# Gates as columns of the first value group, rows by transposes, and five low parts a layer by ScalarE and an adding DMA, in a two-layer hybrid block

## The chip, the cores and the metric

The kernel runs on one core of a Trainium2 chip. The metric is the time of one execution on the device in microseconds, here the median of the runs. One further execution is recorded by the hardware profiler; it has a time of its own, and a span, which goes from the first to the last instruction.

## The reference

Two layers, each a hybrid mixer and a feed-forward part with a convolution, on 512 positions of width 1024. The parts that matter here, cut:

```python
for l in range(2):
    x = x + rms_norm(hybrid_mixer(rms_norm(x, mix_pre_g[l]), w_in[l], ...), mix_post_g[l])
    x = x + rms_norm(conv_ffn(rms_norm(x, ffn_pre_g[l]), ...), ffn_post_g[l])

def hybrid_mixer(hn, w_in, ...):
    # attention q, k, v: 512 columns each; mLSTM q, k, v, o: 512 each; gates: 16
    aq, ak, av, mq, mk, mv, mo, gates = split(hn @ w_in)
    attn = dilated_attention(rotary(aq), rotary(ak), av)          # 8 heads of 64
    mq, mk = silu(depthwise_conv(concat(mq, mk)))
    g = gates + mlstm_gate_b                                      # input and forget gates, 2 directions, 4 heads
    h = mlstm(mq, mk, mv, g, forward) + mlstm(mq, mk, mv, g, backward)
    return concat(attn, rms(h) * head_g * sigmoid(mo)) @ w_out

def conv_ffn(hn, w_up, conv_w, conv_b, w_down):                   # 1024 -> 2 x 2816 -> 1024
    gate, val = split(depthwise_conv(hn @ w_up))
    return (gelu(gate) * val) @ w_down
```

## The kernel before

**Products.** Activations lie with features on partitions and the 512 positions in the free dimension. Each large product is made of three passes in rounded fp32: a number is split in a high part (rounded) and a low part (the rest), and TensorE adds high x high, low x high and high x low. `mac` (L230 to L232) does that for one k-tile of 128: three matmuls with weights standing and 512 positions moving, or 256 where a group is done by halves of the positions.

**Weights** come as 104 pieces a layer (`plan`): 28 of w_in, 8 of w_out, 44 of w_up, 24 of w_down, 512 KB each (128 x 1024). `load_raw` lets SyncE load a piece to `wraw`; `split_w` lets ScalarE cast it to `whi` (L183) and VectorE subtract (`wlo = wraw - whi`, L115). `take` hands the next piece on, and `prefetch(n)` splits up to n pieces ahead, where the code calls it. whi and wlo have rings of three.

**The order of a layer.** `ORDER` gives, for each of four rounds, the order of the mLSTM q and k, the attention q (a) and k (b), and the values (V, two pieces). V has the positions standing and 256 weight columns moving (L923 to L925). `rot_out` turns a and b, `conv_out` does the mLSTM convolution, `v_out` scales V. Two streams (`A` attention, `M` mLSTM with `gates` first) are interleaved with the macs by rates. Beyond that a scheduler fixes each engine's order at build time; an engine then works strictly in its order.

**The first group** of a layer's mixer (`mixer_first`) runs before the norm's scale is known, and the scale is applied to its results. In layer 0 it is gates, q and k for all positions; in layer 1 it follows the feed-forward part of layer 0 and goes by halves, so that the first half starts while the second half of x is still being made; then a is done whole. The gates are products of their own (`gate_macs`, L484 and L486: 16 columns with their low parts as 32 standing columns) in a bank `gps`; `gates` copies them and transposes them (L546).

**The norms.** `Stats` collects squares; `flush` sums them over partitions by small matmuls (L344), `rstd` and `rsqrt_cols` make 1/root on VectorE (rs_y, L282 to L296), `row_of` turns a column into a row spread over all partitions: two fp32 matmuls with `ident_rs`, the identity times 1/RS, since rs_y carries a factor RS (L359). `Post.finish` multiplies that row into the branch (mg or fg, L432), adds it to x (L434) and makes the next operands ah and al (L377, L378). `PreScale.rows` copies the row for the following group (prow). `later` and `settle` put these steps at a count of matmul columns behind the present place (SUM1, ROW1, SUM2, ROW2); gate matmuls aren't counted.

PSUM has eight banks: mm x3, s x2, t x2, o x1.

Of the kernel before, what the change touches and what calls it, by code (L numbers as in the profile page):

```python
# [27 lines left out]
RING = 3  # L28
HD = 128
# [5 lines left out]
ORDER = ["qkaVb", "aqbkV", "qkVab", "qabkV"]  # L35
AR = [.55, None, None, .65]

# [44 lines left out]
def tile_hybrid_block(ctx: ExitStack, tc: tile.TileContext, xt, w_in, w_g, w_out, w_up, w_down, par, cst, out):  # L82
# [8 lines left out]
    wraw_p, whi_p, wlo_p = Lines(big, small, RAW), Lines(big, small, RING), Lines(big, small, RING)  # L91
# [47 lines left out]
    moving = set()  # L139
    for l in range(DEPTH):  # L140
        of = "".join(o.replace("V", "VV") for o in ORDER) + "mmmm"
        for m in range(28):
            if of[m] == "V":
                moving.add(len(plan))
            plan.append(w_in[l, m])
# [10 lines left out]
    def load_raw():  # L156
# [5 lines left out]
        raw = wraw_p.tile([P, 8, P], F32, tag="wraw", name="wraw")  # L162
        nc.sync.dma_start(out=raw[:, 0:nk, :], in_=plan[i])
        raw_q.append((raw, nk, i))

    def split_w(alloc=None):
# [4 lines left out]
        parts = {}  # L171
        n = 8
        k = 0
        while k < nk:
            if alloc is None:

                o = 16 if i in moving else 0
                hi, lo = (q.tile([P, 8 * P + LINE // 4], F32R, tag=t, name=t)[:, o:o + 8 * P].rearrange("p (k c) -> p k c", k=8)
# [5 lines left out]
            lo_part(lo[:, 0:m, :], raw[:, k:k + m, :], hi[:, 0:m, :])  # L184
# [6 lines left out]

    wgs = {}

    def load_gates(l):
        graw = const.tile([P, KT, 16], F32, tag="graw", name="graw")
        nc.sync.dma_start(out=graw, in_=w_g[l])
        g = const.tile([P, KT, 32], F32R, tag="wg", name="wg")
        nc.scalar.copy(out=g[:, :, 0:16], in_=graw)
        lo_part(g[:, :, 16:32], graw, g[:, :, 0:16])
        wgs[l] = g  # L200
# [101 lines left out]
    class Stats:  # L302
# [3 lines left out]
        def __init__(self, own, tag):  # L306
            self.own, self.tag = own, tag
            self.acc = sm.tile([P, T], F32, tag="acc", name="acc")
            self.sp = [None, None]
            self.late = []  # L310

        def add(self, src, n, hf):
# [5 lines left out]
            if hf is None:  # L318
                sq = sm.tile([P, T], F32, tag="sq", bufs=1, name="sq")
# [11 lines left out]
        def flush(self, h):  # L331

            if self.sp[h] is None:
                self.sp[h] = t_ps()
# [45 lines left out]
    class PreScale:  # L380
        def __init__(self, st):
# [3 lines left out]
            self.r = [None, None]  # L385

# [4 lines left out]
        def rows(self, hf):  # L391
            row = row_of(self.r[hf])
            with tc.high_priority():
                nc.scalar.copy(out=self.row[:, halves[hf]], in_=row)
# [6 lines left out]
    class Post:  # L401
# [10 lines left out]
        def put(self, k, src, cols=slice(0, T)):  # L412

            c = PC[self.gname] + k
            nc.scalar.activation(out=self.mg[k][:, cols], in_=src, func=AF.Copy, scale=prm[self.l][:, c:c + 1])
# [9 lines left out]
        def finish(self, hf):  # L425
            cols = halves[hf]
            row = row_of(self.r)
# [47 lines left out]

    def mixer_first(l, xp, sp, G, more, whole=False):
        gps = mm_ps()
        wg = wgs[l]
        ws = [take() for _ in range(G)]
        pss = [mm_ps() if m < 2 else o_ps() for m in range(G)]  # L480
        scale = PreScale(sp() if callable(sp) else sp)

        def gate_macs(k, cols):
            nc.tensor.matmul(out=gps[0:32, cols], lhsT=wg[:, k, 0:32], rhs=xp[k][0][:, cols], start=(k == 0), stop=False,  # L484
                             skip_group_check=True)
            nc.tensor.matmul(out=gps[0:16, cols], lhsT=wg[:, k, 0:16], rhs=xp[k][1][:, cols], start=False,  # L486
                             stop=(k == KT - 1), skip_group_check=True)

        if whole:

            for k in range(KT):
# [3 lines left out]
                gate_macs(k, slice(0, T))  # L495
                for w, ps in zip(ws, pss):
                    mac(ps, w, k, xp[k], k == 0, k == KT - 1)
        else:
            first_group(ws, pss, xp, scale, gate_macs)
        if more:  # L500
            scale.go(1)
            w = take()
            prefetch(RING - 1)
            ps = s_ps()
# [3 lines left out]
            settle(True)  # L508
        return gps, pss, scale, more or whole

    def mixer(l, xp, first, mp, post):
# [18 lines left out]
        gps, pss, scale, more = first  # L530
        st["rt"], st["row"] = scale.rt, scale.row

        def scale_ready():
            settle(True)
            if not more:
                scale.sums(1)
                scale.rows(1)
            nc.vector.tensor_tensor(out=cosr, in0=cosr, in1=scale.row, op=ALU.mult)
            nc.vector.tensor_tensor(out=sinr, in0=sinr, in1=scale.row, op=ALU.mult)

        def gates(ps):
# [5 lines left out]
            gpv = gp[:, 0:P].rearrange("p (c g) -> p c g", c=4)  # L547
            G = mp.tile([P, 4, 16], F32, name="G")
            nc.scalar.copy(out=G, in_=gpv[:, :, 16:32])
            V = nc.vector  # L550
            V.tensor_tensor(out=G, in0=gpv[:, :, 0:16], in1=G, op=ALU.add)
            V.tensor_tensor(out=G, in0=G, in1=st["rt"][:, :].unsqueeze(2).broadcast_to([P, 4, 16]), op=ALU.mult)
            V.tensor_tensor(out=G, in0=G, in1=pr[:, PC["gb"]:PC["gb"] + 16].unsqueeze(1).broadcast_to([P, 4, 16]),
                            op=ALU.add)
# [123 lines left out]
        def v_out(pss):  # L678
# [5 lines left out]
            for b, ps in enumerate(pss):  # L684
# [204 lines left out]

        prefetch(RING - 1)  # L890
        scale_ready()


# [3 lines left out]
        def proj():  # L897
# [4 lines left out]
            ps = mm_ps()  # L902
# [6 lines left out]
        def proj_v():  # L909
# [4 lines left out]
            for c in range(4):  # L914
# [3 lines left out]
                for k in range(KT):  # L918
                    hi, lo = (w[:, 2 * (k % 4):2 * (k % 4) + 2, :].rearrange("p i f -> p (i f)") for w in ws[k // 4])
                    xh, xl = (t[:, c * P:(c + 1) * P] for t in xp[k])  # L920
                    settle()
                    clock[0] += 6 * P
                    nc.tensor.matmul(out=o_, lhsT=xh, rhs=hi, start=(k == 0), stop=False)  # L923
                    nc.tensor.matmul(out=o_, lhsT=xh, rhs=lo, start=False, stop=False)  # L924
                    clock[1] = nc.tensor.matmul(out=o_, lhsT=xl, rhs=hi, start=False, stop=(k == KT - 1)).ins  # L925
# [5 lines left out]
        M.start(gates(gps), .6)  # L931
        for r in range(4):
            done = set()
            for c in ORDER[r]:
                if c == "V":
# [6 lines left out]
                else:  # L942
                    ps = proj()
# [108 lines left out]
    def ffn(l, xp, first, fp, post):  # L1052
# [30 lines left out]
        for m in range(FG, 2 * FT):  # L1083
            if m == FT and l + 1 < DEPTH:
                load_gates(l + 1)
# [56 lines left out]
    load_gates(0)  # L1142
# [16 lines left out]
    prefetch(RING)  # L1159
    for k in range(KT):  # L1160
        sp.add(x[k], k, None)
    ident_rs = const.tile([P, P], F32, name="ident_rs")
    nc.vector.tensor_scalar(ident_rs, ident, 1.0 / RS, None, op0=ALU.mult)
# [3 lines left out]
    for l in range(DEPTH):  # L1167
        with tc.tile_pool(name=f"mix{l}", bufs=1) as mb, tc.tile_pool(name=f"mixs{l}", bufs=1) as ms:
            mp = Lines(mb, ms)
            post = Post(l, "mix_post", l, "ffn_pre", 2)  # L1170
            if first is None:
                first = mixer_first(l, xp, sp, 2, False, True)
# [109 lines left out]
```

## Time and profile before

| | before |
|---|---|
| median of 3 runs | 1354.68 us (1354.65 to 1354.72) |
| profiled execution: time | 1353.89 us |
| profiled execution: span | 1352.0 us |
| TensorE busy | 1323.9 us (98%) |
| VectorE busy | 954.0 us (71%) |
| ScalarE busy | 713.1 us (53%) |
| GpSimd busy | 85.3 us (6%) |
| mean granted clock of TensorE | 0.996 |

The times of the runs and of the profiled execution are from the device; the busy times are shares of the span. In the profile, PE is TensorE, DVE VectorE, ACT ScalarE, POOL GpSimd and SP SyncE. "mm<-ah,whi" names what an instruction writes and reads by the program's names, and "[1.98 <-DVE rs_y L296]" says that it stood idle for 1.98 us before and what ended that.

### The profile page before, as it was taken

How to read it: one execution, taken by the hardware profiler on the slowest of the kernel's cores; microseconds unless marked ns; L12 is line 12 of the kernel's file. 1: busy time of each engine (PE TensorE's matmuls, PEld its weight loads, DVE VectorE, ACT ScalarE, POOL GpSimd, SP SyncE). 2: the span in 40 equal slices, each digit the busy share in tenths (PEclk: the TensorE clock that was granted, in tenths of full speed). 3: DMA queues.
4: the chain of work that ended last, by engine and by line, in shares of the span. 5: the costliest groups of instructions: out<-in, count | busy, mean ns of one | idle time of the engine just before them, and what ended most of it. 6: DMA issues, size and time to landing. Idle time of an engine off the chain costs nothing.

```text
span 1352.0 us, 18666 instructions
## 1 busy us (share of the span) xinstructions
PE 1323.9 (98%) x7152; PEld 1128.6 (83%) x7152; DVE 954.0 (71%) x1901; ACT 713.1 (53%) x1218; POOL 85.3 (6%) x100
## 2 busy tenths in 40 slices
PE   7999999999999999999989999999999999999996
PEld 5888878899888888888978898888998888888886
DVE  6999798847887777422499988887569777773233
ACT  5686696654544444323347867966446444443220
POOL 0000000024000000001130000000320000000002
PEclk9999999999999999999999999999999999999998
DMA  6212112231233332333321122123213333333321
GB/s 238 63 41 86 47 48 79 78 126 44 68 107 96 104 97 90 90 97 111 96 85 51 60 64 65 45 79 99 90 47 96 106 95 94 94 96 96 98 86 63
DMA packets 34089, 115.34 MB, mean 85 GB/s; under 512 B 3664, under 2 KB 6352, under 8 KB 34000
## 3 DMA queue, kind: packets, MB, share of 16 engines
q1 hardware_dynamic: 34000, 114.15, 27.9%
q8 instruction: 56, 0.92, 0.3%
q14 instruction: 33, 0.27, 0.1%
HBM read 112.04 MB, written 2.10 MB: 84 GB/s over the span
## 4 chain that ended last, share of the span: by engine, by line
PE 85%; DVE 7%; ACT 7%; issue 1%; DMA 0%; POOL 0%; SPq 0%; ACTq 0%; DVEq 0%
PE mm L230 18%; PE mm L232 18%; PE mm L231 18%; PE o L230 5%; PE o L231 5%; PE o L232 5%; PE mm L924 2%; PE mm L925 2%; PE mm L923 2%; PE o L786 2%; ACT rb L707 1%; PE t L760 1%; PE t L344 1%; DVE wlo L115 1%; ACT p L752 1%; PE s L743 1%
## 5 line engine op out<-in xcount | busy, mean ns | idle before, releaser
L115 DVE TENSOR_TENSOR wlo<-wraw,whi 128x1024 fp32r<-128x1024 f32 (+1 forms) x192 | 236.5, 1234 | 175.4 <-ACT whi L183 173.3
L230 PE MATMUL mm<-ah,whi 128*128 128x512 f32 (+1 forms) x880 | 337.0, 383 | 0.0
L232 PE MATMUL mm<-al,whi 128*128 128x512 f32 (+1 forms) x880 | 333.2, 380 | 0.8 <-DVE al L378 0.7
L231 PE MATMUL mm<-ah,wlo 128*128 128x512 f32 (+1 forms) x880 | 333.3, 379 | 0.0
L183 ACT CAST whi<-wraw 128x1024 fp32r<-128x1024 f32 (+1 forms) x192 | 198.0, 1035 | 163.2 <-PE mm L232 112.3
L232 PEld LDWEIGHTS mm<-al,whi 128*128 128x128 f32 x880 | 166.2, 189 | 30.8 <-DVE al L378 1.6
L230 PEld LDWEIGHTS mm<-ah,whi 128*128 128x128 f32 x880 | 166.5, 189 | 28.8 <-ACT whi L183 0.5
L231 PEld LDWEIGHTS mm<-ah,wlo 128*128 128x128 f32 x880 | 166.6, 189 | 27.3
L326 POOL TENSOR_TENSOR acc<-acc,sq 128x512 f32<-128x512 f32 x22 | 29.5, 1342 | 1127.0 <-ACT sq L323 1122.6
L230 PE MATMUL mm<-hh,whi 128*128 128x512 f32 x220 | 85.6, 389 | 0.0
L231 PE MATMUL mm<-hh,wlo 128*128 128x512 f32 x220 | 85.6, 389 | 0.0
L232 PE MATMUL mm<-hl,whi 128*128 128x512 f32 x220 | 85.6, 389 | 0.0
L1059 DVE TENSOR_TENSOR u<-mm,prow 128x512 f32<-128x512 f32 x64 | 43.8, 687 | 50.0 <-PE mm L232 39.6
L1076 ACT CAST hh<-cv 128x512 fp32r<-128x512 f32 x44 | 27.3, 620 | 87.6 <-DVE cv L1073 87.6
L923 PE MATMUL mm<-whi,ah 128*128 128x256 f32 x256 | 72.4, 284 | 0.9 <-DVE cu L664 0.9
L924 PE MATMUL mm<-wlo,ah 128*128 128x256 f32 x256 | 71.7, 280 | 0.4 <-DVE wlo L115 0.4
L925 PE MATMUL mm<-whi,al 128*128 128x256 f32 x256 | 71.4, 279 | 0.0
L1071 ACT ACTIVATE cg<-cg 128x512 f32<-128x512 f32 x44 | 27.8, 632 | 74.6 <-DVE cg L1065 74.3
L231 PE MATMUL o<-ah,wlo 128*128 128x512 f32 (+1 forms) x160 | 60.6, 379 | 0.0
L232 PE MATMUL o<-al,whi 128*128 128x512 f32 (+1 forms) x160 | 60.5, 378 | 0.0
L230 PE MATMUL o<-ah,whi 128*128 128x512 f32 (+1 forms) x160 | 60.5, 378 | 0.0
L752 ACT ACTIVATE p<-p,mx 128x512 f32<-128x512 f32 x64 | 46.2, 722 | 18.2 <-DVE mx L749 16.9
(319 smaller groups left out, 2754.9 us busy)
## 6 DMA issues: line engine op xcount, KB each, us to landing
wraw<-in_w_up SPq DMA_DIRECT2D x88, 512.0 KB, 3.6
wraw<-in_w_in SPq DMA_DIRECT2D x56, 512.0 KB, 3.6
wraw<-in_w_down SPq DMA_DIRECT2D x32, 512.0 KB, 3.5
wraw<-in_w_out SPq DMA_DIRECT2D x16, 512.0 KB, 3.6
wraw<-in_w_down SPq DMA_DIRECT2D x16, 384.0 KB, 3.1
x<-in_xt SPq DMA_DIRECT2D x4, 512.0 KB, 7.3
out_dram<-x SPq DMA_DIRECT2D x8, 256.0 KB, 2.1
tb<-in_cst SPq DMA_DIRECT2D x2, 967.0 KB, 5.4
```

Of the source, the lines that this page charges most:

```text
L115: nc.vector.tensor_tensor(out=dst, in0=src, in1=f32v(hi), op=ALU.subtract)
L183: nc.scalar.copy(out=hi[:, 0:m, :], in_=raw[:, k:k + m, :])
L230: nc.tensor.matmul(out=ps, lhsT=hi, rhs=rh, start=first, stop=False)
L231: nc.tensor.matmul(out=ps, lhsT=lo, rhs=rh, start=False, stop=False)
L232: clock[1] = nc.tensor.matmul(out=ps, lhsT=hi, rhs=rl, start=False, stop=last).ins
L326: e.tensor_tensor(out=self.acc[:, cols], in0=self.acc[:, cols], in1=sq, op=ALU.add)
L752: nc.scalar.activation(out=p_, in_=p_, func=AF.Exp, scale=-1.0, bias=mx, accum_out=den)
L923: nc.tensor.matmul(out=o_, lhsT=xh, rhs=hi, start=(k == 0), stop=False)
L924: nc.tensor.matmul(out=o_, lhsT=xh, rhs=lo, start=False, stop=False)
L925: clock[1] = nc.tensor.matmul(out=o_, lhsT=xl, rhs=hi, start=False, stop=(k == KT - 1)).ins
L1059: nc.vector.tensor_tensor(out=u, in0=ps, in1=st["row"], op=ALU.mult)
L1071: nc.scalar.activation(out=g, in_=g, func=AF.Gelu_apprx_tanh)
```

## The change

- The first round's order is "Vqabk". The two value pieces of that round carry the gates: each k-tile has 256 value columns and 16 gate columns (`w_v`, pieces of 128 x 1088), and `value_macs` (L502 to L504) moves 272 columns into four banks, one for each 128 positions (mm x3, o). The gate matmuls, their load and split, the copy and the transposes go; `gates` reads the columns from the four banks, and `v_out` scales from four banks.
- In layer 1 V goes by halves of the positions together with q, which has an s bank; then a has a t bank of its own and runs before the last steps of the scale are settled. In layer 0 V is done whole, then q in an s bank; a has a t bank there too.
- `row_of` makes two transposes with the identity; 1/RS is put into scaled gains (`prs`) and into the copy of prow.
- The two halves' sums of the pre-norm share a bank, the squares have two buffers, whi and wlo rings of four. How far `prefetch` goes is as before.
- For pieces 5 to 9 of each layer (k of the first round, a, q, b, k of the second) ScalarE writes the negated, rounded raw weights to `wlo` (L202), and a DMA issued by GpSimd adds `wraw` to it (L203). VectorE has no part in them.

```diff
-ORDER = ["qkaVb", "aqbkV", "qkVab", "qabkV"]
+ORDER = ["Vqabk", "aqbkV", "qkVab", "qabkV"]
...
-    wraw_p, whi_p, wlo_p = Lines(big, small, RAW), Lines(big, small, RING), Lines(big, small, RING)
+    wraw_p, whi_p, wlo_p = Lines(big, small, RAW), Lines(big, small, RING + 1), Lines(big, small, RING + 1)
...
+            if alloc is None and i % PIECES in range(5, 10):
+
+                nc.scalar.activation(out=lo[:, 0:m, :], in_=raw[:, k:k + m, :], func=AF.Copy, scale=-1.0)
+                nc.gpsimd.dma_start(out=lo[:, 0:m, :], in_=raw[:, k:k + m, :], accum_op=ALU.add)
+            else:
+                lo_part(lo[:, 0:m, :], raw[:, k:k + m, :], hi[:, 0:m, :])
...
-    def row_of(r):
-
-        ps = s_ps()
+    def row_of(r, ps):
+
         for t in range(2):
-            nc.tensor.matmul(out=ps[:, t * P:(t + 1) * P], lhsT=r[:, t:t + 1].broadcast_to([P, P]), rhs=ident_rs,
-                             start=True, stop=True)
-        return ps[:, 0:HW_]
+            nc.tensor.transpose(ps[:, t * P:(t + 1) * P], r[:, t:t + 1].broadcast_to([P, P]), ident)
+        return ps
...
+    def value_macs(out, xk, w, k, cs):
+
+        hi, lo = w
+        for c in cs:
+            xh, xl = (t[:, c * P:(c + 1) * P] for t in xk)
+            settle()
+            clock[0] += 3 * hi.shape[-1]
+            nc.tensor.matmul(out=out[c], lhsT=xh, rhs=hi, start=(k == 0), stop=False)
+            nc.tensor.matmul(out=out[c], lhsT=xh, rhs=lo, start=False, stop=False)
+            clock[1] = nc.tensor.matmul(out=out[c], lhsT=xl, rhs=hi, start=False, stop=(k == KT - 1)).ins
...
         else:
-            first_group(ws, pss, xp, scale, gate_macs)
-        if more:
+            w, ps = take(), s_ps()
+            pss.append(ps)
+            for hf in range(2):
+                for k in range(KT):
+                    if hf == 1 and k == 0:
+                        scale.go(0)
+                    value_macs(vout, xp[k], row(k), k, (2 * hf, 2 * hf + 1))
+                    mac(ps[:, halves[hf]], w, k, xp[k], k == 0, k == KT - 1, halves[hf])
             scale.go(1)
+            late = [t_ps]
+        for place in late:
             w = take()
             prefetch(RING - 1)
-            ps = s_ps()
+            ps = place()
             for k in range(KT):
                 mac(ps, w, k, xp[k], k == 0, k == KT - 1)
             pss.append(ps)
-            settle(True)
-        return gps, pss, scale, more or whole
+        settle(True)
+        return vps, pss, scale
...
-            gs = mp.tile([32, T], F32, tag="sc", name="gs")
-            nc.scalar.copy(out=gs, in_=ps[0:32, :])
-            gp = t_ps()
             for c in range(4):
-                nc.tensor.transpose(gp[:, c * 32:(c + 1) * 32], gs[:, c * P:(c + 1) * P], ident[0:32, 0:32])
...
+                V.scalar_tensor_tensor(out=G[:, c, :], in0=vps[c][:, 2 * P:VC], scalar=st["rt"][:, c:c + 1],
+                                       in1=pr[:, PC["gb"]:PC["gb"] + 16], op0=ALU.mult, op1=ALU.add)
```

How the instructions stand. First TensorE in layer 1's first group, first half, where the row for the second half of layer 0's last norm stands. Before:

```order
L232 MATMUL mm<-al,whi 128x256
L484 MATMUL mm<-ah,wg 32x256
L486 MATMUL mm<-al,wg 16x256
L230 MATMUL mm<-ah,whi 128x256
L231 MATMUL mm<-ah,wlo 128x256
L232 MATMUL mm<-al,whi 128x256
L359 MATMUL s<-ident_rs,rs_y 128x128 x2
L230 MATMUL mm<-ah,whi 128x256
```

After:

```order
L504 MATMUL mm<-whi,al 128x272
L502 MATMUL mm<-whi,ah 128x272
L503 MATMUL mm<-wlo,ah 128x272
L504 MATMUL mm<-whi,al 128x272
L241 MATMUL s<-ah,whi 128x256
L242 MATMUL s<-ah,wlo 128x256
L376 MATMUL s<-c_72,rs_y 128x128 x2
L243 MATMUL s<-al,whi 128x256
L502 MATMUL mm<-whi,ah 128x272
```

The row stood behind 46 matmuls of the group, gates among them, and now stands behind 35, inside the mac of the fourth k-tile.

Next TensorE at the end of the same group (names: s is q's bank, t the bank of a). Before, the last macs are those of a in the s bank, with the second half's row for the pre-norm among them:

```order
L230 MATMUL mm<-ah,whi 128x512
L231 MATMUL mm<-ah,wlo 128x512
L359 MATMUL s<-ident_rs,rs_y 128x128 x2
L232 MATMUL mm<-al,whi 128x512
L230 MATMUL mm<-ah,whi 128x512
```

After:

```order
L502 MATMUL o<-whi,ah 128x272
L503 MATMUL o<-wlo,ah 128x272
L504 MATMUL o<-whi,al 128x272
L241 MATMUL s<-ah,whi 128x256
L242 MATMUL s<-ah,wlo 128x256
L243 MATMUL s<-al,whi 128x256
L376 MATMUL s<-c_72,rs_y 128x128 x2
L241 MATMUL t<-ah,whi 128x512
L242 MATMUL t<-ah,wlo 128x512
```

The first half's row now stands right between the group and a, which is followed by b.

Last GpSimd in layer 0's mixer (klo, mprev and bdg are zeroed buffers of the mixer). Before:

```order
L729 MEMSET klo_295 64x512
L730 MEMSET klo_296 64x512
L618 MEMSET mprev 128x32
L647 MEMSET bdg 64x512
L618 MEMSET mprev 128x32
```

After:

```order
L750 MEMSET klo_370 64x512
L751 MEMSET klo_371 64x512
L634 MEMSET mprev 128x32
L663 MEMSET bdg 64x512
L203 DMA wlo<-wraw 128x1024 x5
L634 MEMSET mprev 128x32
```

The five adding DMAs of a layer stand one behind the other on GpSimd, behind the two memsets of the gates.

## Rows read from the trace of the kernel before

**Rows 1.** The page: busy us, share of the span, instructions of each engine.

```profile
PE 1323.9 (98%) x7152; PEld 1128.6 (83%) x7152; DVE 954.0 (71%) x1901; ACT 713.1 (53%) x1218; POOL 85.3 (6%) x100
```

**Rows 2.** Waits of TensorE, whole span: us in total, times, longest.

```profile
PE mm L484 <- ACT ah L377: 8.2, 3, 6.7
...
PE t L612 <- DVE dgm L609: 0.4, 2, 0.2
```

**Rows 3.** Timeline of TensorE in layer 0's first round: start, duration, instruction.

```profile
29.93 0.39 PE L230 MATMUL mm<-ah,whi 128*128 128x512 f32 x1
...
33.33 0.28 PE L923 MATMUL mm<-whi,ah 128*128 128x256 f32 x1
...
44.64 0.40 PE L230 MATMUL mm<-ah,whi 128*128 128x512 f32 x1
```

**Rows 4.** Timeline of TensorE at the start, to the end of layer 0's first group.

```profile
8.81 0.79 PE L230 MATMUL mm<-ah,whi 128*128 128x512 f32 x1
...
12.13 0.40 PE L232 MATMUL mm<-al,whi 128*128 128x512 f32 x1
...
23.17 0.95 PE L344 MATMUL t<-mean,acc 128*128 128x1 f32 x8
```

**Rows 5.** Timeline of TensorE from layer 1's first matmul to the end of V.

```profile
671.95 0.28 PE L484 MATMUL mm<-ah,wg 128*32 128x256 f32 x1
...
678.30 0.28 PE L232 MATMUL mm<-al,whi 128*128 128x256 f32 x1
680.56 0.74 PE L359 MATMUL s<-ident_rs,rs_y 128*128 128x128 f32 x4 [1.98 <-DVE rs_y L296]
681.03 0.49 PE L230 MATMUL mm<-ah,whi 128*128 128x256 f32 x1
...
694.34 0.31 PE L484 MATMUL mm<-ah,wg 128*32 128x256 f32 x1 [1.10 <-ACT ah L377]
...
703.81 0.36 PE L923 MATMUL mm<-whi,ah 128*128 128x256 f32 x1 [0.86 <-DVE cu L664]
...
715.19 0.40 PE L230 MATMUL mm<-ah,whi 128*128 128x512 f32 x1
```

**Rows 6.** Windows: busy us (instructions) of each engine, granted clock, DMA share, GB/s.

```profile
678.00:681.10 3.10, 1.12 (x9) 0.92 (x9) 2.91 (x9) 1.63 (x4) 1.72 (x2) 1.00 0.01 3
681.10:684.50 3.40, 3.40 (x18) 3.17 (x17) 3.17 (x9) 1.91 (x5) 1.33 (x2) 0.50 0.00 0
```

**Rows 7.** Timeline of TensorE: gates' transposes, row_of, attention's transposes; then row_of's durations.

```profile
28.33 0.43 PE L546 MATMUL t<-c,gs 32*128 32x32 f32 x4
28.68 0.49 PE L230 MATMUL mm<-ah,whi 128*128 128x512 f32 x1
29.02 0.60 PE L359 MATMUL s<-ident_rs,rs_y 128*128 128x128 f32 x4
...
68.07 0.60 PE L760 MATMUL t<-c,p 128*128 128x128 f32 x4
...
L359 PE MATMUL s<-ident_rs,rs_y x64: 270/275/426, 27.2 to 1343.6; 128*128 128x128 f32 x64
```

**Rows 8.** Timeline of VectorE before the row between the layers.

```profile
674.85 0.15 DVE L351 TENSOR_REDUCE ss<-t 128x2 f32<-128x6 f32 x1
...
679.83 0.68 DVE L296 SCALAR_TENSOR_TENSOR rs_y<-rs_a,rs_y 128x2 f32<-128x2 f32 x1
```

**Rows 9.** Groups of the split (busy us, mean ns) and the loads of w_in (median us to landing).

```profile
L115 DVE TENSOR_TENSOR wlo<-wraw,whi 128x1024 fp32r<-128x1024 f32 (+1 forms) x192 | 236.5, 1234 | 175.4 <-ACT whi L183 173.3
L183 ACT CAST whi<-wraw 128x1024 fp32r<-128x1024 f32 (+1 forms) x192 | 198.0, 1035 | 163.2 <-PE mm L232 112.3
wraw<-in_w_in SPq DMA_DIRECT2D x56, 512.0 KB, 3.6
```

**Rows 10.** Windows as in 6, at the front of each layer's mixer.

```profile
25.00:75.00 50.00, 49.49 (x290) 42.17 (x290) 46.97 (x138) 32.17 (x56) 0.13 (x1) 1.00 0.21 64
700.00:750.00 50.00, 48.61 (x285) 40.93 (x284) 47.50 (x126) 34.13 (x59) 0.00 (x0) 1.00 0.26 76
```

More of the change, by code (lines that the diff above doesn't have):

```diff
@@ L28 @@
 RING = 3
+PIECES = 104
 HD = 128
@@ L138, in tile_hybrid_block @@
     plan = []
-    moving = set()
+    moving, gated = set(), set()
     for l in range(DEPTH):
@@ L171, in split_w @@
         parts = {}
+        if i in gated:
+            hi, lo = (q.tile([P, 4 * VC], F32R, tag=t, name=t).rearrange("p (k c) -> p k c", k=4)
+                      for q, t in ((whi_p, "whi"), (wlo_p, "wlo")))
+            nc.scalar.copy(out=hi, in_=raw)
+            lo_part(lo, raw, hi)
+            load_raw()
+            return {"all": (hi, lo)}
         n = 8
@@ L426, in finish @@
             cols = halves[hf]
-            row = row_of(self.r)
+            row = row_of(self.r, s_ps()[:, 0:HW_])
             if not self.final and hf == 0:
@@ L473, in last_tiles, with mixer_first @@
             settle(True)
[L476 to L480, printed above, removed]
-        scale = PreScale(sp() if callable(sp) else sp)
[L483 to L487, printed above, removed]
+    def value_macs(out, xk, w, k, cs):
[7 more added lines that the diff above has]
+            clock[1] = nc.tensor.matmul(out=out[c], lhsT=xl, rhs=hi, start=False, stop=(k == KT - 1)).ins
+    def mixer_first(l, xp, sp, whole=False):
+        ws = [take()["all"] for _ in range(2)]
+        vps = [mm_ps() if c < 3 else o_ps() for c in range(4)]
+        vout = [t[:, 0:VC] for t in vps]
+        scale = PreScale(sp() if callable(sp) else sp)
+        pss = []
+        row = lambda k: [t[:, k % 4, :] for t in ws[k // 4]]
         if whole:
@@ L528, in mixer, with gates @@
         cat = {}
-        gps, pss, scale, more = first
+        vps, pss, scale = first
         st["rt"], st["row"] = scale.rt, scale.row
[L533 to L541, printed above, removed]
-            gs = mp.tile([32, T], F32, tag="sc", name="gs")
-            nc.scalar.copy(out=gs, in_=ps[0:32, :])
-            gp = t_ps()
-            for c in range(4):
-                nc.tensor.transpose(gp[:, c * 32:(c + 1) * 32], gs[:, c * P:(c + 1) * P], ident[0:32, 0:32])
[L547 to L554, printed above, removed]
+        def gates(vps):
+            G = mp.tile([P, 4, 16], F32, name="G")
+            V = nc.vector
+            for c in range(4):
+                V.scalar_tensor_tensor(out=G[:, c, :], in0=vps[c][:, 2 * P:VC], scalar=st["rt"][:, c:c + 1],
+                                       in1=pr[:, PC["gb"]:PC["gb"] + 16], op0=ALU.mult, op1=ALU.add)
             n32 = lambda nm: mp.tile([P, 2, 4, 4], F32, name=nm)
@@ L887, in mlstm, with proj @@
             yield
+        chain = gates(vps)
+        next(chain)
+        v_out(vps)
+        for t in (cosr, sinr):
+            nc.vector.tensor_tensor(out=t, in0=t, in1=st["row"], op=ALU.mult)
         prefetch(RING - 1)
-        scale_ready()
         A = Stream(.5)
         M = Stream(.36)
-        def proj():
+        def proj(place=mm_ps):
             if pss:
@@ L901, in proj @@
             prefetch(RING - 1)
-            ps = mm_ps()
+            ps = place()
             for k in range(KT):
@@ L918, in proj_v @@
                 for k in range(KT):
[L919 to L925, printed above, removed]
+                    w = [w[:, 2 * (k % 4):2 * (k % 4) + 2, :].rearrange("p i f -> p (i f)") for w in ws[k // 4]]
+                    value_macs({c: o_}, xp[k], w, k, (c,))
                     if k % 2:
@@ L929, in proj_v @@
             return vps
-        M.start(gates(gps), .6)
+        M.start(chain, .6)
         for r in range(4):
@@ L942, in mixer @@
                 else:
-                    ps = proj()
+                    ps = proj(t_ps if r == 0 and c == "a" else mm_ps)
                     A.run()
```

79 lines of the change are left out of this document (45 added, 34 removed).

## The prediction

> **What bounds the kernel now.** I read the page first: TensorE is busy 98% of the span, the next engine, VectorE, 71% [rows 1]. Then the waits of TensorE: the list holds about 17 us in nine lines, of which the first and the last stand in [rows 2], and 6.7 us of the first line is the start, before any operand exists. So time can be won in two ways only: TensorE gets less to do, or some of the few waits goes. What TensorE does runs at a fixed step: fifteen matmuls of 512 columns from 29.93 to 33.33 us, 0.227 us each; 96 of 256 columns from there to 44.64, 0.118 us each [rows 3].
>
> Third, the two places that the change rewrites. At the start the gate matmuls come first, behind that wait of 6.7 us; the first matmul with weights of a piece runs at 8.81, when ScalarE has cast them; TensorE's steps are still the double until about 12.1; the group ends at 23.17 [rows 4]. Between the layers [rows 5] the first gate matmul is at 671.95 and the value group ends at 715.19: 43.24 us. The work in it at full step is gates 32 x 0.118 = 3.8, q and k by halves 96 x 0.120 = 11.5, the attention q 24 x 0.227 = 5.4, values 11.3, and small matmuls for sums and rows about 3.1 (of these 0.46 are the gates' transposes): 35.1. The other 8.1 us are stalls: 2.1 at 678.5, where the norm's row waits for rs_y, 1.7 lost to 3.4 us at half clock right behind it [rows 6], 1.2 near 693, 1.0 at 702.8 before the values, the rest in small pieces.
>
> **The change part by part.** *Gates as 16 more columns of V.* A step at 272 columns is on no row; on the line through 0.118 at 256 and 0.227 at 512 it is 0.1246 (estimate), so 96 x 16 columns cost 0.65 us in each layer. In layer 1 the 3.8 us of gate matmuls go: **-3.1**. In layer 0 they (16 of 0.227, 3.6 us) stood partly in time that nothing else could use, so I go by the start. The first piece's cast begins when load and x are there, at best where it does now less the one gate load ahead (0.42 us on SyncE's queue), and takes 1.10 for 1088 columns instead of 1.03: TensorE starts near 8.2. Until 12.1 the steps stay double (0.25 us) and the first low part comes about 1.3 us after the high part: some 15 or 16 of 96 matmuls are done by then. The other 80.5 x 0.1246 = 10.0 end at 22.1 instead of 23.17: **-1.1**. Bounds: 0.3 less only, if the double step lasts as much longer as the work starts thinner; 3.0 less, all that the gates took but the added columns. I take the value between because both ends of the stretch are set by loads and casts, which do not change.
>
> *The gates' transposes* (four a layer, [rows 7]: 0.36 and some 0.1 of restart) go: 0.46 a layer, **-0.5** in layer 0; layer 1's is in the sum between the layers.
>
> *Rows by transposes.* row_of makes two fp32 matmuls, and the trace shows four entries, one 0.11 us behind the other ((0.60 - 0.27) / 3). The transposes of attention also show four entries, at the same step, but for four transposes: one entry each [rows 7]. So two of four entries go, 0.22 us a call, 16 calls: 3.5 in all. Two calls are in layer 0's first group (**-0.4**), three between the layers, eleven elsewhere (**-2.4**). Bounds: nothing (where the row waits for VectorE anyway), and all four entries, 7.0. The Trainium skill says, in "TensorE: Matmul & The Clock Gate", section "Terms", that the transpose mode is four times faster for FP32; by it a call would save 0.33 us and the sixteen 5.3, where the rows' factor of two gives 3.5. No run here shows a factor of four.
>
> *Between the layers.* Work: 3.1 less for the gates; 0.3 less because one piece instead of two goes by halves (48 x 0.120 against 24 x 0.227); 0.7 for three rows; 0.5 for the gates' transposes. That leaves V with gates 12.0, q by halves 5.8, a and b 10.9, small matmuls 1.9: about 30.5. Waits: the row that waits today comes in the new order after 35 matmuls of the group (first pair of order rows), some 4.4 us of work from its first matmul; today it is 6.6 us (671.95 to 678.58). Its rs_y is a VectorE chain that runs between other VectorE work from 674.85 to 680.51 [rows 8]; with one product of the operands less ahead of it I place its end near 679, 7.0 us from the first matmul. The small matmuls of the sums and a wait of 0.5 ahead of them come to some 0.9 us, so the row waits about 7.0 - 4.4 - 0.9 = 1.7 to 1.8 us; the half clock after it I count at 45% of 1.7 us; 0.5 before the sums, 0.5 in small pieces: 3.6 instead of 8.1. The chain behind the row, to the last operand of the half at 694.34 [rows 5], takes 13.3 us (from 681.03); TensorE has some 13 us of work behind the new row before it needs that (4.4 of the first half, 8.9 of the second less its end), so it about fits. The wait of 1.0 before V goes because V is first and has its banks. In sum 30.5 + 3.6 = 34.1 against 43.24: **-9.1** (3.1 + 0.3 + 0.7 + 0.5 + 4.5).
>
> *Low parts by ScalarE and an adding DMA.* Ten subtractions of 1.23 us leave VectorE, 12.3 us; ScalarE gets ten casts of 1.03 [rows 9]. They stand where VectorE is busiest: 47 of 50 us, while TensorE is busy 49.5 and 48.6 of 50 [rows 10]. So there is little for TensorE to win: I take **0**, bounds 4 less (the small waits of the mixers that end on VectorE) and 2 more (a later order of ScalarE's casts: 32 of 50 us busy and 5 more cover it). The DMA costs no engine on the path, if it lands in time. Its price is on no row: no DMA issued by GpSimd is in this trace. It reads and writes as much as the 512 KB loads do, which take 3.6 us from issue to landing [rows 9]; above, three such times, 11 us. The tightest piece is layer 1's k: its negative is written about 12.5 us before TensorE needs it, since a and b, 5.4 us each, stand between. I take it as hidden.
>
> Sum: 1.1 + 0.5 + 0.4 + 9.1 + 2.4 = 13.5. The profiled execution has a span of 1352.0 and a time of 1353.89; 13.5 less is 1338.5 and 1340.4. The median of the runs, 1354.68, is 0.8 above the profiled one, so I predict **1341.2 us**.
>
> **The rivals.**
> *1. The adding DMA is late (slower).* TensorE then waits at the matmul with the low part of pieces 5 to 9. With L us from ScalarE's write to landing, each layer loses L - 12.5 once, as the five transfers follow one another at TensorE's own step of 5.4 us a piece. 2 x (L - 12.5) eats the 13.5 at L = 19.3; at L = 22 the time is 1341.2 + 19 = 1360. Against: a load of the same size lands in 3.6. For: an accumulating transfer reads both sides, and its issue is new on GpSimd. "DMA: Bandwidth & Descriptors", section "SWDGE vs HWDGE vs iDMA", of the Trainium skill says that GpSimd writes such a transfer's descriptors into SBUF state that VectorE can lock it out of; that would make L long just where VectorE is busy 94%. No run here shows it. The same page's section "Anatomy of one DMA" gives 2.0 us plus bytes over 436 GB/s, an estimate of 3.2 us here, which keeps it hidden.
> *2. The row's wait between the layers grows.* TensorE reaches the row 2.2 us earlier. If rs_y stays where it is, at 680.5, the wait is 3.3 instead of 1.8 and the half clock comes for sure (+0.9): 1341.2 + 2.4 = 1343.6. For: VectorE's chain is untouched, and VectorE is busy 2.9 of the 3.1 us there [rows 6].
> *3. The stalls move on.* The 4.5 us of stalls and 1.1 us of the start come back as waits at the front of the mixers, where VectorE is nearly full [rows 10] and now reads four banks instead of two: only less work counts, 13.5 - 5.6 = 7.9, and the time is 1346.8.
> *4. More is won.* VectorE's relief ends the mixers' small waits: 4 us more, 1337.2.
>
> **How the numbers follow.** Chances: forecast 0.52, rival 2 0.17, rival 3 0.15, rival 4 0.06, rival 1 0.10 (of it 0.07 at L above 19, 0.03 around it). The range goes from 1336.5, a little past rival 4, to 1350, past rival 3 by the 3 us of the bounds on the start and VectorE; it leaves out rival 1. What a measurement can tell from no change is about 0.2%, 2.7 us. Faster 0.87: all but rival 1 and 0.03 for a loss that I did not see; within it 0.05 and slower 0.08, these two from rival 1's parts and that rest.
>
> **What would show it.** Right: the new first group steps at 0.125 us; layer 0's ends near 22.1; a row's run of transposes is two entries; from layer 1's first matmul to the end of V, q, a and b 34 us; VectorE is below 43 of 50 us in 25 to 75. Wrong: waits of the low parts' matmuls on a DMA (rival 1); a wait over 3 us at the row in layer 1 with a stretch at half clock (rival 2); new waits of TensorE on VectorE in the first 50 us of a mixer (rival 3).

## The result and the profile after

The changed kernel takes **1344.74 us** in the median (1344.47 to 1345.1, 4 runs) against 1354.66 us before: ratio 0.993, 95% interval 0.9918 to 0.9942. That is 9.9 us less. The forecast was 1341.2, 13.5 less, with a range from 1336.5 to 1350: the way and the range hold, the gain is a quarter short.

The page's busy times, which answer to [rows 1], and TensorE's longest waits, which answer to [rows 2]:

```profile
PE 1311.0 (98%) x7040; PEld 1117.6 (83%) x7040; DVE 942.5 (70%) x1892; ACT 724.9 (54%) x1230; POOL 93.4 (7%) x110
...
PE mm L502 <- ACT whi L184: 8.9, 1, 8.9
PE s L376 <- DVE rs_y L307: 4.1, 4, 1.8
PE mm L503 <- DVE wlo L119: 2.2, 2, 1.6
```

The line of before that answers to the third wait:

```profile
PE mm L924 <- DVE wlo L115: 0.4, 2, 0.2
```

TensorE is still busy 98% and lost 12.9 us of work. No wait for a DMA stands in the list. The third line has grown from 0.4 to 2.2 us: TensorE waits for VectorE's low parts of a value group.

To see where a gain of this size went, cut both traces at TensorE's landmarks (the first instruction of each stage, but for the first cut of before) and compare piece by piece. All times are us of the two profiled executions:

| stage of TensorE | before | after | difference | forecast |
|---|---|---|---|---|
| start of the span to the end of layer 0's first group | 24.5 | 23.7 | -0.8 | -1.1 |
| rest of layer 0's mixer, to the first matmul of w_out | 231.5 | 228.3 | -3.2 | -0.9 |
| w_out, layer 0 | 47.7 | 48.2 | +0.5 | -0.2 |
| feed-forward, layer 0 | 368.3 | 367.5 | -0.7 | -0.9 |
| layer 1: V and three more pieces | 43.2 | 35.1 | -8.2 | -9.1 |
| rest of layer 1's mixer | 208.9 | 212.6 | +3.6 | 0 |
| from layer 1's w_out to the end | 419.5 | 418.7 | -0.8 | -1.3 |
| sum | | | -9.6 | -13.5 |

The first cut of before needs care. At 23.17 the group isn't at its end, as [rows 4] and the prediction have it: 42 of its 48 matmuls for q and k have started, and the other six stand behind the first of the norm's sums (small matmuls), the last of them at 26.11:

```profile
23.98 0.49 PE L230 MATMUL mm<-ah,whi 128*128 128x512 f32 x1
...
26.11 0.39 PE L232 MATMUL mm<-al,whi 128*128 128x512 f32 x1
```

Six matmuls of 0.227 us are 1.4 us, so the table takes 24.5 for the group's work; the sums count in the second row, before and after.

So the sum hides two errors with opposite signs, in the two mixers: 3.6 us lost in layer 1's, 2.3 more won in layer 0's. The stage that was argued most closely, between the layers, came out within 1 us. Its rows, TensorE's timeline, which answer to [rows 5]:

```profile
667.74 0.29 PE L502 MATMUL mm<-whi,ah 128*128 128x272 f32 x1
...
669.21 0.61 PE L362 MATMUL t<-mean,sqp 128*128 128x1 f32 x4 [0.56 <-ACT sqp L335]
...
674.94 0.40 PE L376 MATMUL s<-c,rs_y 128*128 128x128 f32 x2 [1.47 <-DVE rs_y L307]
...
689.01 0.39 PE L502 MATMUL mm<-whi,ah 128*128 128x272 f32 x1 [0.45 <-ACT ah L393]
...
702.82 0.39 PE L241 MATMUL mm<-ah,whi 128*128 128x512 f32 x1
```

V, q, a and b end at 702.82, 35.1 us behind the first matmul. The waits are close to those of the forecast: 0.56 before the sums (0.5 said), 1.47 at the row (1.7 to 1.8), and 0.45 at an operand of the second half, where the forecast had 0.5 in small pieces. The stretch at half clock behind the row [rows 6] is gone: the steps of 272 columns behind 674.94 are 0.125 us and the window from 676 to 680 has a granted clock of 1.00.

Some 45 us behind that, inside layer 1's mixer, the same timeline shows what was given back:

```profile
748.11 0.28 PE L502 MATMUL mm<-whi,ah 128*128 128x256 f32 x1
750.00 0.38 PE L503 MATMUL mm<-wlo,ah 128*128 128x256 f32 x1 [1.61 <-DVE wlo L119]
...
752.21 0.47 PE L863 MATMUL s<-bdm,lu 128*128 128x512 f32 x1 [0.58 <-DVE lu L861]
...
757.03 0.39 PE L503 MATMUL mm<-wlo,ah 128*128 128x256 f32 x1 [0.64 <-DVE wlo L119]
```

And the windows of layer 1's front (columns as in [rows 6]) show that VectorE had been idle 3.8 of 13 us not long before:

```profile
690.00:703.00 13.00, 13.00 (x67) 10.96 (x66) 9.21 (x33) 11.05 (x20) 2.81 (x3) 1.00 0.88 213
...
715.00:730.00 15.00, 14.79 (x75) 11.82 (x74) 14.48 (x51) 13.57 (x27) 0.12 (x1) 1.00 0.28 70
730.00:750.00 20.00, 18.26 (x114) 15.32 (x112) 18.60 (x41) 17.11 (x33) 0.00 (x0) 1.00 0.00 1
```

The start, which answers to [rows 4]:

```profile
8.86 1.05 PE L502 MATMUL mm<-whi,ah 128*128 128x272 f32 x3 [8.86 <-ACT whi L184]
...
14.21 0.43 PE L502 MATMUL o<-whi,ah 128*128 128x272 f32 x1
14.43 0.33 PE L503 MATMUL o<-wlo,ah 128*128 128x272 f32 x1
14.60 0.29 PE L504 MATMUL o<-whi,al 128*128 128x272 f32 x1
...
23.74 0.39 PE L241 MATMUL s<-ah,whi 128*128 128x512 f32 x1
```

Steps are 0.227 us until 14.4 and 0.125 behind (72 from 14.72 to 23.74). 272 columns in 0.227 us is 1.2 GHz. Before, the doubled steps ended at 12.1.

### The profile page after: what moved, and what is told of

It reads as the page before. It is cut to its first block, busy times and chain, and to the rows that moved or that the text cites. A ratio compares the mean times of both kernels' runs of the same rounds, so it can differ in the third digit from the quotient of the medians.

```text
span 1342.3 us, 18531 instructions
## 1 busy us (share of the span) xinstructions
PE 1311.0 (98%) x7040; PEld 1117.6 (83%) x7040; DVE 942.5 (70%) x1892; ACT 724.9 (54%) x1230; POOL 93.4 (7%) x110
## 4 chain that ended last, share of the span: by engine, by line
PE 85%; ACT 7%; DVE 5%; DMA 1%; issue 1%; POOL 1%; SPq 0%; POOLq 0%; ACTq 0%
PE mm L243 18%; PE mm L241 18%; PE mm L242 18%; PE o L241 5%; PE o L243 5%; PE o L242 5%; PE o L807 2%; PE mm L503 2%; PE mm L504 2%; PE mm L502 2%; PE t L781 1%; PE s L764 1%; ACT pth L784 1%; PE t L362 1%; ACT rb L728 1%; PE s L765 1%
## 5 line engine op out<-in xcount | busy, mean ns | idle before, releaser
L119 DVE TENSOR_TENSOR wlo<-wraw,whi 128x1024 fp32r<-128x1024 f32 (+2 forms) x182 | 223.8, 1232 | 181.2 <-ACT whi L199 173.5
L241 PE MATMUL mm<-ah,whi 128*128 128x512 f32 (+1 forms) x832 | 319.3, 384 | 0.3
L242 PE MATMUL mm<-ah,wlo 128*128 128x512 f32 (+1 forms) x832 | 317.3, 382 | 0.0
L243 PE MATMUL mm<-al,whi 128*128 128x512 f32 (+1 forms) x832 | 316.4, 381 | 0.8 <-DVE al L394 0.8
L243 PEld LDWEIGHTS mm<-al,whi 128*128 128x128 f32 x832 | 156.2, 188 | 30.0 <-DVE al L394 1.6
L242 PEld LDWEIGHTS mm<-ah,wlo 128*128 128x128 f32 x832 | 156.7, 188 | 26.7
L502 PE MATMUL mm<-whi,ah 128*128 128x256 f32 (+1 forms) x240 | 69.3, 290 | 9.3 <-ACT whi L184 8.9
L503 PE MATMUL mm<-wlo,ah 128*128 128x256 f32 (+1 forms) x240 | 68.6, 286 | 2.3 <-DVE wlo L119 2.2
L504 PE MATMUL mm<-whi,al 128*128 128x256 f32 (+1 forms) x240 | 68.3, 285 | 0.0
L502 PEld LDWEIGHTS mm<-whi,ah 128*128 128x128 f32 x240 | 45.8, 192 | 10.2 <-ACT whi L184 8.9
```

What stands on the lines that cost most here:

```text
L119: nc.vector.tensor_tensor(out=dst, in0=src, in1=f32v(hi), op=ALU.subtract)
L241: nc.tensor.matmul(out=ps, lhsT=hi, rhs=rh, start=first, stop=False)
L242: nc.tensor.matmul(out=ps, lhsT=lo, rhs=rh, start=False, stop=False)
L243: clock[1] = nc.tensor.matmul(out=ps, lhsT=hi, rhs=rl, start=False, stop=last).ins
L502: nc.tensor.matmul(out=out[c], lhsT=xh, rhs=hi, start=(k == 0), stop=False)
L503: nc.tensor.matmul(out=out[c], lhsT=xh, rhs=lo, start=False, stop=False)
```

## The experiments

Twelve kernels, in three groups of four, each timed in five rounds with the kernel before (whose medians in the three groups were 1354.55, 1354.57 and 1354.18). The changed kernel was timed apart from them, beside 1354.66. An interval of a ratio is about 0.0012 either way, 1.6 us, so differences between two edited kernels below 2 us lean on the trace as well as on the times. No experiment puts the gates or the old order back: the stage between the layers is read from the two traces alone.

### What each part is worth

**lo_dve**: all low parts by VectorE.

```diff
-            if alloc is None and i % PIECES in range(5, 10):
+            if alloc is None and i % PIECES in range(0):
```

> The changed kernel with all low parts by VectorE again (no adding DMA, no ScalarE negatives). Theory 1: the 3.6 us that layer 0's mixer won come from VectorE's relief, and layer 1's mixer, where TensorE now waits for VectorE's low parts of V, would wait longer without it: 3.5 us more in layer 0 and 2 to 4 more in layer 1, so 1350 to 1352. Rival: the new order at the front of the mixer won them and the relief is worth nothing: 1344 to 1346, the waits of layer 1's second V as they are (about 3.3 us).

Measured 1347.44 (0.995, 0.9937 to 0.9962): the adding DMA is worth about 2.7 us. By stages the rest of layer 0's mixer is 229.7 (after 228.3, before 231.5) and layer 1's whole mixer 250.4 (after 247.6, before 252.2). So in this execution, 0.75 us above the median, the relief pays 1.4 us in layer 0 and 2.8 in layer 1. The 2.8 aren't all waits for VectorE: from 754 to 762 us the granted clock is 0.79 here, up to 1.7 us, and the changed kernel has no such stretch. Of layer 0's 3.2 us some 1.8 are there without the relief. Neither theory holds whole.

**before_dma**: the kernel before with the adding DMA alone (the same two new lines in its `split_w`).

> The kernel before, with only the last part of the change: ScalarE's negatives and the adding DMA for pieces 5 to 9 of each layer. Theory 1: VectorE's relief ends small waits of the mixers in any order: 3 to 6 us less, 1349 to 1352. Rival: in the old order TensorE hardly waits for VectorE there, and the relief only pays once the group before is shorter: 1354 to 1355.

Measured 1354.42 (1.0, 0.9991 to 1.0009): nothing. The rival was right: the relief of 12 us of VectorE's time has no worth of its own in the old order. That it needs a front that runs ahead of VectorE is the likely reason; the ring of three low parts, which this kernel keeps, was not tried apart.

**row_mm**: rows by plain matmuls.

```diff
-            nc.tensor.transpose(ps[:, t * P:(t + 1) * P], r[:, t:t + 1].broadcast_to([P, P]), ident)
+            nc.tensor.matmul(out=ps[:, t * P:(t + 1) * P], lhsT=r[:, t:t + 1].broadcast_to([P, P]), rhs=ident,
+                             start=True, stop=True)
```

> The changed kernel with row_of's two transposes as two plain fp32 matmuls with the same identity; results are scaled as in the changed kernel. If an entry costs 0.11 us wherever it stands: 32 entries more, 3.5 us, 1348.2. If rows that stand behind a wait cost nothing (about 5 of 16 calls do): 2.4 us, 1347.1. If a transpose is four times cheaper and not twice: 5.3 us, 1350.0.

Measured 1349.19 (0.9965, 0.9952 to 0.9977): 4.5 us more. One call in TensorE's timeline, here first and in the changed kernel below:

```profile
29.92 0.61 PE L376 MATMUL s<-c,rs_y 128*128 128x128 f32 x4
30.29 0.48 PE L241 MATMUL s<-ah,whi 128*128 128x512 f32 x1
```

```profile
30.38 0.38 PE L376 MATMUL s<-c,rs_y 128*128 128x128 f32 x2
30.51 0.48 PE L241 MATMUL s<-ah,whi 128*128 128x512 f32 x1
```

Four entries take 0.36 us to the next matmul, two take 0.13: 0.23 a call, 3.6 for sixteen. The other 0.9 lie inside the measurement; the profiled execution also has a granted clock of 0.83 from 750 to 760 us, where the changed kernel has 1.00.

**a_late**: layer 1's a out of the first group.

```diff
-            late = [t_ps]
+            late = []
```

> The changed kernel in which layer 1's a is no part of the first group: the last steps of the scale are settled behind V and q, and a follows in the mixer's own code (in the same bank). If a covers the wait for the second half's scale, as the forecast took it: TensorE waits some 3 us for rs_y behind the group, 1347 to 1348. If VectorE's idle time there is what counts: the scale comes earlier, and it ends near 1342 to 1343. If the scheduler mixes a's matmuls in anyway, without either effect: 1344 to 1345.

Measured 1343.22 (0.9917, 0.9903 to 0.993): 1.5 less than the changed kernel, the same within the interval. The scheduler still runs a's first matmuls ahead, and the row stands among them. TensorE's timeline:

```profile
695.15 0.40 PE L376 MATMUL s<-c,rs_y 128*128 128x128 f32 x2 [2.30 <-DVE rs_y L307]
```

So TensorE pays 2.3 us for the early scale here, and the granted clock behind it is 0.66 from 695 to 700 us, some 1.7 us more. Yet layer 1's mixer is only 0.8 us longer (248.4): about 3 us come back behind it. Of the changed kernel's waits at 750 to 757 us (1.6, 0.6 and 0.6) none is left, as VectorE got the scale sooner. a does cover a wait of that size, as the forecast took it. The first theory's time is excluded; 1343.22 lies between the ranges of the other two, and both of their mechanisms show.

### Where the missing gain went

**sum_early**: in layer 1 the second half's sums and row earlier within a: the sums at 691.13 where they were at 693.48, the row at 694.79 where it was at 697.15.

```diff
-            scale.go(1)
+            scale.go(1, sum2=SUM2 // 4, row2=ROW2 * 3 // 8)
```

> The changed kernel with the second half's sums of layer 1's first norm two products earlier in a (behind one of its eight, not four) and the row behind five of eight and not at the end: nothing but TensorE's order in that one place. Theory 1: VectorE's idle time from 690 to 703 us is what it lacks at 748: it gets the scale 2 to 2.5 us earlier, the waits of TensorE behind it (0.9 at 712, 1.8 at 748, 0.7 at 751, 0.8 at 756) shrink by about as much: 1342 to 1343. Rival: TensorE then waits for the last squares ahead of the sums, or VectorE is bound by its amount: 1344 to 1345.

Measured 1342.61 (0.9912, 0.9899 to 0.9926): 2.1 less. VectorE's window shows the cause:

```profile
690.00:703.00 13.00, 13.00 (x67) 10.89 (x66) 11.91 (x37) 12.34 (x21) 1.99 (x2) 1.00 0.83 201
```

It is busy 11.9 us where it was 9.2, TensorE has no wait here, and layer 1's mixer takes 245.6 instead of 247.6. The wait of 1.6 at the V group's low part is gone; the longest wait on VectorE or ScalarE from 690 to 780 us is 0.4. Theory 1 holds.

**dma12**: the second V's two pieces by the adding DMA too.

```diff
-            if alloc is None and i % PIECES in range(5, 10):
+            if alloc is None and i % PIECES in range(5, 12):
```

> The changed kernel with seven adding DMAs a layer instead of five: also the two pieces of the second round's V. Theory 1: layer 1's mixer gives 3.5 us back because VectorE has too much to do there (TensorE waits 1.6 and 0.6 us for VectorE's low parts of just these pieces, and 0.6 for the mLSTM's lu): two subtractions of 1.2 us less, those waits go, 2 to 3 us less, 1342 to 1343. Rival: VectorE is late by the order and not by the amount (it stood idle 3.8 of 13 us from 690 to 703): the wait moves to the mLSTM, less than 1 us won; or the DMA, 4.4 to 7.1 us to landing, is now what V waits for: 1344 to 1347.

Measured 1341.96 (0.9911, 0.9897 to 0.9924): 2.8 less. Layer 1's mixer takes 244.5, and of TensorE's waits from 690 to 780 us only small ones are left:

```profile
PE t L597 <- issue: 0.7, 1, 0.7
PE s L863 <- DVE lu L861: 0.2, 1, 0.2
PE t L628 <- DVE dgm L625: 0.2, 1, 0.2
```

Both cures work, one by time (VectorE starts sooner), one by amount (it has less to do). So what layer 1 gave back was VectorE's lateness at that V group, the forecast's rival 3 in one of the two layers.

**row_late**: the row of the post-norm later.

```diff
-SUM1, ROW1, SUM2, ROW2 = [int(t * 2400) for t in (0.6, 3.3, 2, 8)]
+SUM1, ROW1, SUM2, ROW2 = [int(t * 2400) for t in (0.6, 4.2, 2, 8)]
```

> The changed kernel with the row of the post-norm 2160 columns later in TensorE's order (ROW1 4.2 for 3.3), in all four places. Theory 1: the 1.6 us that TensorE waits at the row between the layers are covered by nothing because the chain behind the row (13 us of VectorE and GpSimd) bounds the stretch: the row still goes out when rs_y is there, the wait comes back later at the last operands, within 0.7 us of the changed kernel: 1344 to 1345. Rival: a wait filled is a wait won, 1.6 between the layers and two of 0.5 in each feed-forward group: 1342 to 1343.

Measured 1351.77 (0.998, 0.9972 to 0.9989): 7.0 us **more**. The mechanism was right, the price far too low. The timeline and the windows behind it:

```profile
676.46 0.41 PE L376 MATMUL s<-c,rs_y 128*128 128x128 f32 x2 [1.35 <-DVE fg L451]
...
691.50 0.40 PE L504 MATMUL mm<-whi,al 128*128 128x272 f32 x1 [3.00 <-DVE al L394]
...
690.00:693.00 3.00, 1.50 (x8) 1.50 (x9) 2.72 (x10) 0.91 (x3) 1.09 (x2) 0.80 0.91 324
693.00:696.00 3.00, 3.00 (x15) 2.90 (x15) 0.73 (x3) 1.53 (x3) 0.24 (x1) 0.63 0.38 152
```

The wait at the row did not even go: the first half's row is late as well, and the second needs the bank that VectorE still reads for the first (the releaser is now fg). The operands come later, TensorE waits 3.0 us for the last, and the granted clock falls to 0.63 behind that. The two feed-forward groups, which had two waits of 0.4 us each, get one of 1.3 us each at their first matmul, and a lower clock behind it (0.91 from 300 to 320 us, where the changed kernel has 1.00). Layer 1's mixer takes 251.8, 4.2 of the 7 us. A wait at the head of a chain that bounds the stretch is not to be filled.

### The start

**warm**: matmuls of ones ahead of the first piece.

```diff
+    warm = t_ps()
+    for _ in range(20):
+        nc.tensor.matmul(out=warm[:, 0:P], lhsT=ones, rhs=ones, start=True, stop=True)
```

> The changed kernel with 20 matmuls of ones by ones (128 columns, a bank that nobody reads) ahead of the first piece on TensorE. Theory 1: the doubled step of 0.227 us from 8.86 to 14.4 us goes with TensorE's first work, so it passes while TensorE would be idle: the first group runs at 0.126 from the start, as far as operands allow, and ends near 21.6 instead of 23.74: 1342.5. Rival: the stretch is bound by the casts and products that feed it (VectorE is busy 5.35 of 5.44 us there): it ends within 0.5 us of 23.74, with waits in place of long steps, 1344.5.

Measured 1343.08 (0.9914, 0.9901 to 0.9928): 1.7 less. TensorE's timeline:

```profile
1.00 6.48 PE L1174 MATMUL t<-ones 128*128 128x128 f32 x40 [1.00 <-POOL mean L134]
9.06 0.64 PE L502 MATMUL mm<-whi,ah 128*128 128x272 f32 x3 [1.58 <-ACT whi L184]
9.54 0.28 PE L502 MATMUL o<-whi,ah 128*128 128x272 f32 x1
10.38 0.39 PE L503 MATMUL mm<-wlo,ah 128*128 128x272 f32 x1 [0.56 <-DVE wlo L119]
...
22.03 0.39 PE L241 MATMUL s<-ah,whi 128*128 128x512 f32 x1
```

The group starts no sooner and ends at 22.03, since its steps are 0.125 us from the second on. The casts bind it only by the 0.56 at the first low part. The slow steps are in the early matmuls instead: their 40 entries stand 0.21 us apart up to 4.6 us and 0.11 behind that. So the doubled steps go with TensorE's first work after the start: gates before, V after, ones here.

### Is the adding DMA near the path?

**dma_x2** and **dma_x3**: one, or two, plain copies of the low part onto itself behind each adding DMA, so that it is ready that much later. The values stay as they are.

```diff
                 nc.gpsimd.dma_start(out=lo[:, 0:m, :], in_=raw[:, k:k + m, :], accum_op=ALU.add)
+                for _ in range(2):
+                    nc.gpsimd.dma_start(out=lo[:, 0:m, :], in_=lo[:, 0:m, :])
```

> The changed kernel with a second transfer behind each adding DMA, which copies the low part onto itself, so that it is ready one transfer later (L from 6 to some 11 or 12 us). By the 12.5 us of cover that the forecast counted, it is just hidden: 1344.5 to 1346. If the cover is shorter, 2 to 6 us more.

> The same with two such copies: L some 17 or 18 us. By the forecast's rival 1 each layer loses L - 12.5 once: 2 x 5 = 10 us more, 1355, with waits of TensorE on a DMA at the low parts of pieces 5 to 9. If the five transfers do not overlap (one queue, one after the other), every piece waits: 20 us more and above. If prefetch holds them earlier than counted: under 4 us more.

Measured 1344.79 (0.9926, 0.9913 to 0.9938), no change with one wait of 0.6 us on the copy, and 1355.67 (1.001, 1.0001 to 1.0019), 10.9 more. The third transfer brings the wait that rival 1 described, in TensorE's list:

```profile
PE mm L244 <- DMA wlo<-wlo: 10.0, 2, 7.6
```

Two waits, one in each layer, 10.0 us together; two times 5 were forecast. They aren't equal (2.4 and 7.6): the cover in layer 1 is the shorter, as said. Behind the longer one the granted clock is 0.57 from 710 to 718 us, and TensorE's later waits on VectorE shrink (2.2 to 1.3 at the second V's low parts), so the agreement of the 10.9 with the 10 is in part luck. In the changed kernel the ten adding DMAs have this landing, and with 12.5 us of cover and 5 to 7 of landing they are hidden with a transfer's time to spare:

```profile
L203 POOL DMA_DIRECT2D wlo<-wraw x10: 859/869/1073, 25.2 to 714.3; - x10
...
DMA to landing us min/median/max: 4.4/5.3/7.1
```

### The edits together

**all3**: warm, sum_early and dma12 in one kernel.

> The changed kernel with the three edits that each won alone: the 20 early matmuls at the start (1.7 won), seven adding DMAs a layer (2.8), the second half's sums and row earlier in layer 1's a (2.1). If the last two win from the same waits of layer 1's second V (3.3 us in all), they overlap: 1.7 + 2.8 + 0.5 to 1 = 5 to 5.5 less, 1339 to 1340. If they win apart: 6.6 less, 1338.

Measured 1341.28 (0.9902, 0.9888 to 0.9915), 3.5 less than the changed kernel: the lowest median, though within the measurement of dma12's, and less gain than the sum that was expected. The overlap of the last two is as said or stronger (layer 1's mixer 245.5, no better than either alone). The start's 1.7 us are mostly missing too in the execution profiled; its windows from 9 us show where:

```profile
9.00:12.00 3.00, 2.44 (x15) 2.22 (x15) 3.00 (x4) 3.00 (x6) 0.00 (x0) 0.83 1.00 388
12.00:16.00 4.00, 4.00 (x26) 4.00 (x25) 3.92 (x7) 4.00 (x8) 0.00 (x0) 0.70 1.04 375
```

The granted clock falls again between 11 and 14.4 us: the early matmuls end at 7.2, and TensorE then waits 1.55 and 0.56 us before the group is in step. The group ends at 23.27. warm had the same two waits without the fall, so what decides it isn't shown.

**all3_dma11**: the same with `range(5, 16)`, eleven pieces.

> As the kernel with the three edits, but eleven adding DMAs a layer (pieces 5 to 15, all to the third round's V). If VectorE still is what TensorE waits for in the mixers: 1 to 2 us less again, 1337 to 1338.5. If the last waits there are ScalarE's or the streams' own chains, or ScalarE gets too much: no better, 1339 to 1341.

Measured 1342.15 (0.9908, 0.9893 to 0.9923): no better. Here the clock held at the start (the group ends at 21.83), and the mixers lost it again: layer 0's rest takes 230.3, layer 1's mixer 245.8. More than seven pieces won nothing. A longer run of early matmuls, up to the first cast, was not tried.

## Why the prediction was right, and where it was not

By its number the forecast was in part lucky. 1344.74 lies nearer to rival 3's price (1346.8) than to 1341.2, and 2.7 of the 9.9 us came from a part that the sum held at 0. Of the five signs of being right three came: the step, the two entries and the stage between the layers (35.1 for 34). Layer 0's group ended later than 22.1, and VectorE was busy 44.1 of 50 us, not below 43.

**Gates as columns.** Right in layer 1, both the step (0.1246 forecast, 0.125 measured) and the stage. In layer 0 two steps of the prediction failed, and they nearly cancel, by luck. The first is "Until 12.1 the steps stay double", because "both ends of the stretch are set by loads and casts". The doubled steps are not fixed in time. They begin with TensorE's first matmul: from 6.74 to 12.1 before, where the gates come first, and from 8.86 to 14.4 after, where V does. Five of the 16 gate matmuls ran in the slow steps, four of them before the first matmul with weights of a piece; the other eleven cost 0.227 us each. The start of TensorE at 8.2 was missed as well: the pieces of 544 KB land late enough that the cast begins at 7.71, where it began before. So by the nine profiled executions with this start the group ends between 22.5 and 23.9, the middle one at 23.1, and not at 22.1. The second is "instead of 23.17": six of the group's matmuls come behind that, and its work goes to 24.5 (24.8 in before_dma). The term is thus about -1.5 us, -0.8 in the execution of the table, where -1.1 was forecast; with the right end of before the forecast's own steps would have said -2.4.

**Rows by transposes.** Right: two entries of four, 0.23 us a call. The Trainium skill gives a factor of four for FP32 in "TensorE: Matmul & The Clock Gate", section "Terms"; by it a call would have saved an estimated 0.33 us and left one entry, and the runs show two entries and 0.23. The time of row_mm, 4.5 give or take 1.6, does not tell 3.5 from 5.3; the entries do.

**Between the layers.** Right within 1 us; the half clock that was counted at 45% did not come. The waits are 2.5 us by the rows shown (2.8 forecast without the clock), and the work with its restarts takes 32.6 instead of 30.5: the one term of this stage that was too small, by 2.1. Rival 2 did not come.

**Low parts by the adding DMA.** Hidden, as forecast; the bound of 11 us held (7.1 at most). The term that took its worth as 0 was too small, though inside its bounds: it is worth 2.7 us in the changed kernel and nothing in the old order. The rows of the old order [rows 10] could not show it, likely because there TensorE did not yet run ahead of VectorE. The landing is 5.3 us in the median. The Trainium skill's fit in "DMA: Bandwidth & Descriptors", section "Anatomy of one DMA", gave an estimate of 3.2 us. Its sentence against this part, in section "SWDGE vs HWDGE vs iDMA" of the same page, did not decide anything here: the longer landing stayed hidden, and no run tells whether VectorE's lock or the second read makes the difference.

**The mixers, taken as unchanged.** The forecast has them at 0 but for gates and rows, and that was wrong twice. Layer 1 lost 3.6 us, rival 3 in one layer: TensorE arrives 8 us earlier, VectorE doesn't, and three waits of V and the mLSTM follow, 2.8 us together; sum_early and dma12 each take most of that away. Layer 0 won 3.2 where 0.9 was forecast. Of the other 2.3 some 0.4 is plain work that the sum left out: V's 96 steps of 0.118 us moved from the mixer into the first group, and q's and k's 48 of 0.227 moved the other way. Of the 1.9 left lo_dve lacks 1.4, so most of it goes with VectorE's relief in the new order. TensorE's waits in this stage went from 2.3 to 1.5 us, and lo_dve has 2.5 of them; among those that ended are 0.7 and 0.5 for r and hs of the mLSTM's first head inside the second V. These are single executions, and kernels with the same code there differ by up to 0.8 us, so a finer account stays open.

## What to carry to other kernels

When the engine that bounds a kernel is made faster in one stage, look for the next engine's idle time behind that stage: here two microseconds came back by putting a sum and a row 2.4 us earlier, and an edit that had no worth in the old order was worth 2.7 in the new one. A wait at the head of a chain that bounds a stretch must not be filled with other work: in layer 1's mixer the head went out 1 us later, and it cost 4. And before work is removed from the start, ask what it did for the clock. When two traces are cut at a landmark, count the work on either side of it: here six matmuls behind it were worth 1.4 us.

## What was unexpected of the hardware

TensorE's steps were double (272 columns in 0.227 us, 1.2 GHz) at its first work, gates, V or ones; the profile's column of the granted clock reads 1.00 in that first stretch, so there it is read from the steps. In one execution a run of early matmuls, a pause of 1.55 us and another of 0.56 were followed by double steps again (granted clock 0.83 and 0.70); after pauses of 1.58 and 0.56 in a second, and 1.06 and 0.56 in a third, they were not.

An adding DMA of 512 KB from GpSimd landed in 4.4 to 7.1 us and occupied GpSimd for 0.87 us; a load of the same size by SyncE took 3.6. The standing operand of a transpose loads in 0.134 us where that of the fp32 matmul takes 0.190.
